# Six more projections by half products, sums kept in PSUM, and tiles moved to other start addresses

## The chip, the cores and the metric

The kernel runs on one core of one Trainium2 chip. The metric is device microseconds of one execution. Three timed runs of the kernel before gave 1398.69, 1399.0 and 1400.92 us, a median of 1399.0 us.

## The reference

One layer of a decoder with four branches, on 256 tokens of width 2048, in float32. `xn` is the normalised input; one large input matrix is cut into columns of 1024 (and four of 2048).

```
(a_q, a_k, a_v, a_g, c_b, c_c, c_h, c_g, s_q, s_k, s_v, s_g, m_q, m_g,
 i_q, i_k, i_w, r_a, r_c, r_s, r_m) = [xn @ w for w in cols]
y_a = moba_attention(a_q, a_k, a_v) * silu(a_g)        # 8 heads x 128, block branch
y_c = c_b * short_conv(c_c * c_h, conv_w, conv_b) * silu(c_g)
y_s = dsa_attention(s_q, s_k, s_v, i_q, i_k, i_w) * silu(s_g)
y_m = memory_attention(m_q, mk, mv) * silu(m_g)
merged = (sigmoid(r_a) * (y_a @ w_branch[0]) + sigmoid(r_c) * (y_c @ w_branch[1])
        + sigmoid(r_s) * (y_s @ w_branch[2]) + sigmoid(r_m) * (y_m @ w_branch[3]))
return rms_norm(x + merged @ w_out, final_g)
```

`short_conv` is a causal convolution of width 3 along the tokens, channel by channel.

## The kernel before

All weights (some 260 MB) stream once from HBM, 1 MB at a time (a tile `raw`, four buffers), on SP's queue. Every matrix product is made of three passes: ACT copies a half `raw` into `hi` (128x1024, type fp32r, line 104), DVE makes `lo = raw - hi` (line 105), both in tiles with four buffers, and PE sums hi·hi, hi·lo and lo·hi in PSUM. The activations (`x_hl`) lie split in the same way.

There are three ways to project 1024 columns:

- *Transposed* (`project_t`, lines 142 to 151): the weights are stationary, the 256 tokens move. 8 blocks of 128 columns x 16 chunks of depth x 3 passes are 384 matmuls of 256 columns. The result comes with channels on the partitions, which the attention and the convolution want. The queries, keys and gates and the convolution's four (C_C, C_H, C_B, C_G) go this way; their rows name the PSUM tile `acc`.
- *Natural* (`project`, lines 163 to 177): the activations are stationary, 512 columns of weights move. 2 halves of tokens x 2 halves of columns x 16 chunks x 3 passes are 192 matmuls of 512 columns. Rows name `r`, `v`, `w` (branch matrices) and `o` (output matrix).
- *By halves* (`by_halves`, lines 222 to 270): as natural, but over the first half of the depth the 2x2 blocks are multiplied with seven products instead of eight, from sums of activations (`x_sums`, made once) and differences of weight quarters (DVE, lines 241, 245, 251 and 261). 7x12 + 96 = 180 matmuls of 512 columns. The partial products `m` (one bank at a time) are added up in SBUF by DVE (lines 248, 249, 254, 255), then come `z`, `r`, `x` and `y` (lines 258 and 269). Seven projections go this way.

A stage of a branch is: queries, keys, values, attention (spread over the gate's projection), the gate (`to_gate`), and twice for j = 0, 1 the columns of `gate_columns` and their `merge` with the branch matrix. The first `gate_columns` of the branches M, S and A is natural, all others go by halves. The branches come in the order M, S, A, C. The order of instructions within an engine is set by the scheduler of the tile framework from the order of the code and its own estimates.

Tiles of one pool lie one behind the other. `u` (line 609) is 8x258x4 = 8256 bytes per partition, 64 more than a multiple of 128, so the tiles that lie behind it (`y`, `raw`, `hi`, `lo`) start 64 bytes off those before it (`x_hl`, `x_sums`, `mt`), counted modulo 128. The operands of a `w` matmul (`y`, `hi`) both lie behind it; those of `r`, `o` and of the halved ones lie on either side.

Of the kernel before, what the change touches and what calls it, by code (L numbers as in the profile page):

```python
# [9 lines left out]
F32 = mybir.dt.float32  # L10
# [26 lines left out]
SECTIONS_T = [(c, W) for c in (M_Q, M_G, S_Q, S_K, S_G, A_Q, A_K, A_G, C_C, C_H, C_B, C_G)]  # L37
SECTIONS_N = [(S_V, W), (A_V, W), (R_0, 4 * D)]
# [6 lines left out]
TOPK = 64  # L45


@with_exitstack
def hybrid_kernel(ctx, tc, x, xT, mem, memT, ln_g, mem_ln_g, w_t, w_n, w_idx, conv_w, conv_b, w_mem_k, w_mem_v,
# [26 lines left out]
    cb = const.tile([P, 8], F32, name="cb")  # L76
    nc.gpsimd.dma_start(out=g_x, in_=ln_g)
# [79 lines left out]
    def products(o, ah, al, hi, lo, start, stop):  # L157

        nc.tensor.matmul(o, lhsT=ah, rhs=hi, start=start, stop=False)  # L159
        nc.tensor.matmul(o, lhsT=ah, rhs=lo, start=False, stop=False)  # L160
        nc.tensor.matmul(o, lhsT=al, rhs=hi, start=False, stop=stop)  # L161
# [60 lines left out]
    def by_halves(srcs, act, sums, nat, done):  # L222
# [3 lines left out]
        (n00, n10), (n01, n11) = ([part(nat, t, n) for t in range(2)] for n in range(2))  # L226

# [38 lines left out]
        for k0 in (8, 12):
            plain((y, x), act, srcs[0], k0, (False, False), (k0 == 12,) * 2)
        for t, (o, i) in enumerate(((n00, y), (n10, x))):
            nc.vector.tensor_add(o, i, o)
# [444 lines left out]
```

## Time and profile before

| | |
|---|---|
| median of three timed runs | 1399.0 us |
| profiled execution, its own time | 1398.06 us |
| its span, first to last instruction | 1396.3 us |
| PE busy | 1380.4 us, 99% |
| DVE busy | 933.4 us, 67% |
| ACT busy | 729.2 us, 52% |
| granted TensorE clock, mean | 0.997 |

Busy time of PE counts a matmul from its start to its modelled end, and these overlap: a matmul of 256 columns has a duration of 280 ns, and the next begins 113 to 118 ns after it. So what a matmul costs is read from the distance between starts, or from a window's length over its count. A duration of DVE or ACT can be taken as it stands.

### The profile page before, as it was taken

To read this page: it belongs to the slowest core of one execution; us is meant where nothing else is said; L and a number is where in the kernel's file an instruction comes from. 1 tells how busy PE (TensorE), PEld (TensorE's weight loads), DVE (VectorE), ACT (ScalarE), POOL (GpSimd) and SP (SyncE) were. 2 spreads that over 40 slices of the span, in tenths; PEclk is the share of its full clock that TensorE was granted. 3 is DMA by queue.
4 is the path that set the end of the run, shared out by engine and by line. 5 is a ranking of instruction groups with operands and counts; after the bars stand their busy time and mean duration, and the time that the engine had idled before them with its cause. 6 is when DMAs were issued, how large, how long until landed. Compare 5 with 4: busy or idle time off the path is not lost.

```text
span 1396.3 us, 21263 instructions
## 1 busy us (share of the span) xinstructions
PE 1380.4 (99%) x8796; PEld 1243.9 (89%) x8796; DVE 933.4 (67%) x1123; ACT 729.2 (52%) x991; POOL 11.0 (1%) x25
## 2 busy tenths in 40 slices
PE   9999999999999999999999999999999999999997
PEld 9998998789998898878999899878999998878887
DVE  7687764774848884596546885487547558787654
ACT  7663675453445684354445585445343345545443
POOL 1000000000000000000000000000000000000000
PEclk9999999999999999999999999999999999999999
DMA  9774545375554735537553746537555654736551
GB/s 343 291 271 173 191 156 180 128 266 189 172 197 133 254 128 183 189 135 247 188 193 133 243 150 211 182 125 266 183 181 187 225 192 148 265 130 241 183 197 73
DMA packets 49969, 269.49 MB, mean 193 GB/s; under 512 B 6656, under 2 KB 17456, under 8 KB 19024
## 3 DMA queue, kind: packets, MB, share of 16 engines
q1 hardware_dynamic: 48960, 264.03, 55.0%
q0 software_dynamic: 624, 3.31, 0.6%
q8 instruction: 69, 1.13, 0.3%
q10 hardware_dynamic: 288, 0.79, 0.1%
q14 instruction: 28, 0.23, 0.0%
HBM read 265.88 MB, written 2.10 MB: 192 GB/s over the span
## 4 chain that ended last, share of the span: by engine, by line
PE 85%; DVE 8%; DMA 3%; issue 2%; ACT 2%; SPq 0%; POOLq 0%; POOL 0%; DVEq 0%; ACTq 0%
PE acc L138 13%; PE acc L140 13%; PE acc L139 13%; DVE lo L105 5%; PE w L160 4%; PE w L161 4%; PE w L159 4%; PE r L159 4%; PE r L161 4%; PE r L160 4%; PE o L160 2%; PE o L161 2%; PE o L159 2%; DMA raw<-in_w_n 1%; PE y L160 1%
## 5 line engine op out<-in xcount | busy, mean ns | idle before, releaser
L105 DVE TENSOR_TENSOR lo<-raw,hi 128x1024 fp32r<-128x1024 f32 (+1 forms) x538 | 640.0, 1202 | 416.5 <-ACT hi L104 414.4
L104 ACT CAST hi<-raw 128x1024 fp32r<-128x1024 f32 (+1 forms) x538 | 552.2, 1032 | 547.8 <-PE acc L139 196.4
L139 PE MATMUL acc<-x_hl,hi 128*128 128x256 f32 x1520 | 426.0, 280 | 0.0
L138 PE MATMUL acc<-x_hl,hi 128*128 128x256 f32 x1520 | 425.4, 280 | 0.5 <-ACT qt L155 0.5
L140 PE MATMUL acc<-x_hl,lo 128*128 128x256 f32 x1520 | 425.8, 280 | 0.0
L140 PEld LDWEIGHTS acc<-x_hl,lo 128*128 128x128 f32 x1520 | 288.1, 190 | 0.1
L138 PEld LDWEIGHTS acc<-x_hl,hi 128*128 128x128 f32 x1520 | 284.8, 187 | 0.9 <-ACT qt L155 0.7
L139 PEld LDWEIGHTS acc<-x_hl,hi 128*128 128x128 f32 x1520 | 284.8, 187 | 0.2
L159 PE MATMUL w<-hi,y 128*128 128x512 f32 x256 | 99.9, 390 | 0.0
L161 PE MATMUL w<-hi,y 128*128 128x512 f32 x256 | 99.7, 389 | 0.0
L160 PE MATMUL w<-lo,y 128*128 128x512 f32 x256 | 99.6, 389 | 0.0
L159 PE MATMUL r<-hi,x_hl 128*128 128x512 f32 x248 | 98.3, 396 | 0.0
L161 PE MATMUL r<-hi,x_hl 128*128 128x512 f32 x248 | 97.9, 395 | 0.0
L160 PE MATMUL r<-lo,x_hl 128*128 128x512 f32 x248 | 97.6, 394 | 0.0
L159 PEld LDWEIGHTS w<-hi,y 128*128 128x128 f32 x256 | 48.1, 188 | 10.0
L161 PEld LDWEIGHTS w<-hi,y 128*128 128x128 f32 x256 | 48.1, 188 | 10.0
L160 PEld LDWEIGHTS w<-lo,y 128*128 128x128 f32 x256 | 48.1, 188 | 9.9
L161 PEld LDWEIGHTS r<-hi,x_hl 128*128 128x128 f32 x248 | 46.7, 188 | 10.6
L160 PEld LDWEIGHTS r<-lo,x_hl 128*128 128x128 f32 x248 | 46.7, 188 | 10.4
L159 PEld LDWEIGHTS r<-hi,x_hl 128*128 128x128 f32 x248 | 46.9, 189 | 10.2
L161 PE MATMUL o<-hi,mt 128*128 128x512 f32 (+1 forms) x160 | 55.3, 347 | 0.0
L160 PE MATMUL o<-lo,mt 128*128 128x512 f32 (+1 forms) x160 | 55.1, 346 | 0.0
(246 smaller groups left out, 1860.7 us busy)
## 6 DMA issues: line engine op xcount, KB each, us to landing
raw<-in_w_t SPq DMA_DIRECT2D x92, 1024.0 KB, 5.0
raw<-in_w_n SPq DMA_DIRECT2D x80, 1024.0 KB, 4.9
raw<-in_w_branch SPq DMA_DIRECT2D x32, 1024.0 KB, 5.3
raw<-in_w_out SPq DMA_DIRECT2D x16, 1024.0 KB, 4.8
raw<-in_w_mem_k SPq DMA_DIRECT2D x8, 1024.0 KB, 6.4
raw<-in_w_mem_v SPq DMA_DIRECT2D x8, 1024.0 KB, 5.5
raw<-in_w_t SPq DMA_DIRECT2D x16, 256.0 KB, 5.9
raw<-in_memT SPq DMA_DIRECT2D x2, 1024.0 KB, 8.8
```

Source lines behind the costliest of these rows:

```text
L104: nc.scalar.copy(out=hi, in_=src)
L105: nc.vector.tensor_sub(out=lo, in0=src, in1=hi.bitcast(F32))
L138: nc.tensor.matmul(o, lhsT=hi, rhs=a[:, 0], start=(k == 0), stop=False)
L139: nc.tensor.matmul(o, lhsT=hi, rhs=a[:, 1], start=False, stop=False)
L140: nc.tensor.matmul(o, lhsT=lo, rhs=a[:, 0], start=False, stop=(k == nk - 1))
L159: nc.tensor.matmul(o, lhsT=ah, rhs=hi, start=start, stop=False)
L160: nc.tensor.matmul(o, lhsT=ah, rhs=lo, start=False, stop=False)
L161: nc.tensor.matmul(o, lhsT=al, rhs=hi, start=False, stop=stop)
```

## The change

- The block branch's queries and keys and the convolution's C_C, C_H, C_G and C_B go by halves, in natural layout. Queries, keys, the product C_C*C_H and the product C_B*silu(C_G) are then brought to channels on partitions by 16 transposes of 128x128 each (`transposed`).
- The first `gate_columns` of S and A, and two of the output matrix's four column blocks, go by halves too; for the latter, sums of the merged activations are made (`m_sums`).
- `by_halves` keeps its running sum in PSUM: `u` takes three products one on top of the other and is copied out by ACT in between; `m`, `x`, `y` go on collecting. DVE adds once for each of the four results (`finish`). Differences of weights go into tiles of their own (`held`: h1, h2), in place of a tile that is free at that time.
- Start addresses: `u`'s tile becomes 8704 bytes, a small tile `fill` shifts all that follows, and the weight parts start 64 bytes later where they are stationary. Now both operands of every 512-wide matmul start at the same place modulo 128, and those of the transposed form 64 bytes apart, as before.

```diff
-SECTIONS_T = [(c, W) for c in (M_Q, M_G, S_Q, S_K, S_G, A_Q, A_K, A_G, C_C, C_H, C_B, C_G)]
-SECTIONS_N = [(S_V, W), (A_V, W), (R_0, 4 * D)]
+SECTIONS_T = [(c, W) for c in (M_Q, M_G, S_Q, S_K, S_G, A_G)]
+SECTIONS_N = [(c, W) for c in (S_V, A_Q, A_K, A_V, C_C, C_H, C_G, C_B)] + [(R_0, 4 * D)]
+STATIONARY = 64
+    fill = const.tile([P, 56], F32, name="fill")
-    def parts_tiles(w=NB, c=NB):
-        return [spl.tile([P, 2 * NB], F32R, name=n, tag=n).rearrange("p (k c) -> p k c", c=w)[:, :, :c]
-                for n in ("hi", "lo")]
+    def parts_tiles(w=NB, c=NB, place=0):
+        i = place // 4
+        return [spl.tile([P, 2 * NB + 64], F32R, name=n, tag=n)[:, i:i + 2 * NB]
+                .rearrange("p (k c) -> p k c", c=w)[:, :, :c] for n in ("hi", "lo")]
...
-                hi, lo = parts_tiles(w, c)
+                hi, lo = parts_tiles(w, c, STATIONARY if w == TB else 0)
...
+        held = [big.tile([P, 8 // len(room) * NB], F32, name="held", tag=r) for r in room]
...
+        def finish(o, t, n):
+            p = part(nat, t, n)
+            nc.vector.tensor_add(p, o, p)
+            done(t, n, p, False)
         b11 = quarter(srcs[0], 0)
-        m1 = bank("m", tag)
-        product(m1, a(0, 0), b11, True, True)
-        nc.scalar.copy(out=n00, in_=m1)
-        z, r = bank("z", other), bank("r", other)
-        plain((z, r), act, srcs[1], 8, (True, True), (False, False))
+        u = bank("u", tag)
+        product(u, a(0, 0), b11, True, True)
+        nc.scalar.copy(out=n00, in_=u)
+        x, y = bank("x", other), bank("y", other)
+        plain((y, x), act, srcs[0], 8, True, False)
         b12 = quarter(srcs[1], 0)
-        nc.vector.tensor_sub(out=b11, in0=b12, in1=b11)
-        m5 = bank("m", tag)
-        product(m5, s(0), b11, True, True)
+        nc.vector.tensor_sub(out=h1, in0=b12, in1=b11)
+        m = bank("m", tag)
+        product(m, s(0), h1, True, True)
+        nc.scalar.copy(out=n11, in_=m)
+        plain((y, x), act, srcs[0], 12, False, False)
         b22 = quarter(srcs[1], 4)
-        nc.vector.tensor_sub(out=b11, in0=b22, in1=b11)
-        m6 = bank("m", tag)
-        product(m6, s(1), b11, True, True)
-        nc.vector.tensor_add(n10, m6, n00)
-        nc.vector.tensor_add(n01, m5, n10)
-        plain((z, r), act, srcs[1], 12, (False, False), (False, True))
-        nc.vector.tensor_sub(out=b12, in0=b22, in1=b12)
-        m7 = bank("m", tag)
-        product(m7, s(2), b12, True, True)
-        nc.vector.tensor_add(n10, m7, n10)
-        nc.vector.tensor_add(n11, m7, n01)
-        product(z, s(3), b22, False, True)
+        nc.vector.tensor_sub(out=h1, in0=b22, in1=h1)
+        product(u, s(1), h1, False, True)
+        nc.scalar.copy(out=n01, in_=u)
+        nc.vector.tensor_sub(out=h2, in0=b22, in1=b12)
+        product(u, s(2), h2, False, True)
+        nc.scalar.copy(out=n10, in_=u)
+        product(m, s(3), b22, False, False)
+        plain((m, u), act, srcs[1], 8, False, False)
         b21 = quarter(srcs[0], 4)
+        nc.vector.tensor_sub(out=h1, in0=b21, in1=h1)
+        product(x, a(1, 1), h1, False, True)
+        finish(x, 1, 0)
+        plain((m, u), act, srcs[1], 12, False, True)
+        product(y, a(1, 0), b21, False, True)
+        finish(m, 0, 1)
+        finish(u, 1, 1)
+        finish(y, 0, 0)
...
+    def transposed(nat, done):
+        for c in range(0, 8, 2):
+            pp = halves(bank("tp", "s"))
+            for i in range(2):
+                for t in range(2):
+                    nc.tensor.transpose(pp[:, i, t * P:(t + 1) * P], nat[:, t, (c + i) * P:(c + i + 1) * P], ident)
+            done(c, pp)
...
-    q = to_heads("qt", A_Q)
-    k = to_heads("kt", A_K)
+    q = to_heads("qt", A_Q, True)
+    k = to_heads("kt", A_K, True)
...
+    uu = nat_tile("uu", "vv")
+    columns(C_C, uu, kept(uu), True)
+    nat = nat_tile("ch")
+    columns(C_H, nat, times(nat, uu), True)
+    u = big.tile([P, 8 * (T + 16)], F32, name="u", tag="kt")[:, :8 * (T + 2)].rearrange("p (c t) -> p c t", c=8)
+    transposed(uu, lambda c, pp: nc.scalar.copy(out=u[:, c:c + 2, 2:], in_=pp))
...
+    bg = nat_tile("bg", "vv")
+    columns(C_G, bg, through(bg, AF.Silu), True)
+    nat = nat_tile("cb")
+    columns(C_B, nat, times(nat, bg), True)
+    y = y_parts()
+    transposed(bg, lambda c, pp: gate_parts(y, yt_tile(), pp, cc, c))
...
-    finish(BR_C, C_G, cc, (True, True), after=parts_of)
+    finish(BR_C, y, after=parts_of, last=merged_sums)
+    sums_of(lambda k0, n: mt[:, k0:k0 + n], m_sums[0])
...
+        by_halves([w_out[1], w_out[2]], lambda k: mt[:, k], m_sums[0], nat,
+                  lambda t, n, src, psum: got.append((1 + n, t, src)), ("y",))
```

`times` multiplies a result on DVE into the tile of its partner; `gate_parts` multiplies two transposed channels blocks with the convolution's result and splits them into `y`'s parts.

PE, where the halved keys' projection follows the halved queries': eight transposes of the queries (`nqt`) stand amid the products `x`, `y` and `m` of the next call.

```order
L168 MATMUL x<-hi,x_hl 128x512
L166 MATMUL y<-hi,x_hl 128x512
L166 MATMUL x<-hi,x_hl 128x512
L342 MATMUL tp<-ident,nqt 128x128 x8
L166 MATMUL m<-hi,x_sums 128x512
L167 MATMUL y<-lo,x_hl 128x512
```

Before, no transposes stood here, and nothing but matmuls of 256 columns.

PE again, in a halved call of the change: the end of the second product on `u`, one matmul of `m`, and the third product on `u`. Line 265's copy of `u` by ACT lies between the two.

```order
L166 MATMUL u<-hi,x_sums 128x512
L167 MATMUL u<-lo,x_sums 128x512
L168 MATMUL u<-hi,x_sums 128x512
L166 MATMUL m<-hi,x_sums 128x512
L166 MATMUL u<-hi,x_sums 128x512
L167 MATMUL u<-lo,x_sums 128x512
```

Before, the two products went to different banks, with matmuls of `z` and `r` ahead of the second; now the bank is the same and one matmul lies between.

DVE, where the convolution stands: first before, among the weight parts `lo` of the projection C_H, 2 + 1 + 3 instructions of it (lines 617 and 619) between parts that serve 256-wide matmuls.

```order
L614 TENSOR_TENSOR u<-acc,qt 128x256 x2
L617 TENSOR_SCALAR qt<-u,cw,cb 128x256 x2
L619 SCALAR_TENSOR_TENSOR qt<-u,cw,qt 128x256
L105 TENSOR_TENSOR lo<-raw,hi 128x1024
L619 SCALAR_TENSOR_TENSOR qt<-u,cw,qt 128x256 x3
L105 TENSOR_TENSOR lo<-raw,hi 128x1024 x3
```

Now, in the halved call for C_G, between two differences of weights (lines 266 and 263) and the third (line 272):

```order
L263 TENSOR_TENSOR held<-raw,held 128x2048
L110 TENSOR_TENSOR lo<-raw,hi 128x1024
L658 TENSOR_SCALAR cc<-u,cw,cb 128x256 x8
L110 TENSOR_TENSOR lo<-held,hi 128x1024
L660 SCALAR_TENSOR_TENSOR cc<-u,cw,cc 128x256 x2
L110 TENSOR_TENSOR lo<-held,hi 128x1024
L660 SCALAR_TENSOR_TENSOR cc<-u,cw,cc 128x256 x3
L110 TENSOR_TENSOR lo<-held,hi 128x1024
L660 SCALAR_TENSOR_TENSOR cc<-u,cw,cc 128x256 x3
L110 TENSOR_TENSOR lo<-held,hi 128x1024
L660 SCALAR_TENSOR_TENSOR cc<-u,cw,cc 128x256 x2
L272 TENSOR_TENSOR held<-raw,held 128x2048
```

All 24 instructions of the convolution (18 of them above, six behind line 272) moved from a stage of transposed projections into the middle of one halved call, between the parts that the products on `u` and `m` wait for.

## Rows read from the trace of the kernel before

**Rows 1.** The page's first part: busy time, its share of the span, instructions.

```profile
PE 1380.4 (99%) x8796; PEld 1243.9 (89%) x8796; DVE 933.4 (67%) x1123; ACT 729.2 (52%) x991; POOL 11.0 (1%) x25
```

**Rows 2.** The page's chain of work that ended last, shares of the span by engine.

```profile
PE 85%; DVE 8%; DMA 3%; issue 2%; ACT 2%; SPq 0%; POOLq 0%; POOL 0%; DVEq 0%; ACTq 0%
```

**Rows 3.** Windows cut at stage edges: from:to, length, then busy us (and instructions) of PE, PEld, DVE, ACT and POOL, granted clock, DMA share, GB/s. In order: block branch's queries and keys (transposed); the convolution's four (transposed); first gate columns of S and of A (natural, a few matmuls of edges and attention in the count); three 512-wide blocks of the output matrix.

```profile
665.40:755.80 90.40, 90.40 (x769) 90.40 (x768) 43.83 (x39) 38.02 (x49) 0.00 (x0) 1.00 0.53 181
987.10:1168.00 180.90, 180.90 (x1538) 180.90 (x1537) 100.95 (x115) 73.98 (x83) 0.54 (x1) 1.00 0.55 189
531.90:576.70 44.80, 44.80 (x195) 36.29 (x194) 20.83 (x18) 20.49 (x23) 0.00 (x0) 1.00 0.55 182
854.80:899.60 44.80, 44.80 (x194) 36.30 (x193) 20.82 (x18) 20.50 (x23) 0.00 (x0) 1.00 0.60 205
...
1300.00:1366.00 66.00, 66.00 (x294) 54.27 (x293) 36.94 (x38) 28.80 (x34) 0.00 (x0) 1.00 0.51 176
```

**Rows 4.** The same view for the seven halved projections, each cut from its first matmul to the next stage's first: one with attention matmuls in it (S_V), the longest, the shortest, and the view's last line, which sums and averages all seven.

```profile
432.90:476.00 43.10, 42.88 (x194) 35.02 (x193) 38.29 (x40) 26.52 (x32) 0.00 (x0) 1.00 0.60 208
598.50:643.60 45.10, 43.54 (x181) 34.76 (x180) 38.94 (x37) 24.36 (x25) 0.00 (x0) 0.96 0.58 198
...
1168.00:1210.40 42.40, 42.06 (x183) 33.47 (x182) 37.33 (x35) 26.08 (x29) 0.53 (x1) 1.00 0.67 236
...
sum 303.70, PE 297.93 PEld 238.73 DVE 267.38 ACT 175.44 POOL 0.53; mean PE 42.56 PEld 34.10 DVE 38.20 ACT 25.06 POOL 0.08
```

**Rows 5.** Timeline of PE, start us and duration, four pairs, each the first and the last of a run of matmuls: ten transposed ones in the convolution's stage, ten in the stage of S's queries, seven of the form `r`, seven of the form `w`.

```profile
1049.83 0.28 PE L140 MATMUL acc<-x_hl,lo 128*128 128x256 f32 x1
...
1050.89 0.28 PE L140 MATMUL acc<-x_hl,lo 128*128 128x256 f32 x1
...
399.79 0.28 PE L140 MATMUL acc<-x_hl,lo 128*128 128x256 f32 x1
...
400.81 0.28 PE L140 MATMUL acc<-x_hl,lo 128*128 128x256 f32 x1
...
549.62 0.40 PE L160 MATMUL r<-lo,x_hl 128*128 128x512 f32 x1
...
551.02 0.40 PE L160 MATMUL r<-lo,x_hl 128*128 128x512 f32 x1
...
909.82 0.39 PE L159 MATMUL w<-hi,y 128*128 128x512 f32 x1
...
911.18 0.39 PE L159 MATMUL w<-hi,y 128*128 128x512 f32 x1
```

**Rows 6.** Groups of instructions by line in the window 1168.0 to 1210.4, one halved call (DVE, then ACT): parts, a difference of weights, an addition onto the result, ACT's part, ACT's copy out of PSUM. Columns: busy us, mean ns of one, idle before.

```profile
L105 DVE TENSOR_TENSOR lo<-raw,hi 128x1024 fp32r<-128x1024 f32 x23 | 27.3, 1220 | 4.7 <-ACT hi L104 4.6
...
L245 DVE TENSOR_TENSOR raw<-raw 128x2048 f32<-128x2048 f32 x1 | 2.3, 2285 | 0.0
...
L249 DVE TENSOR_TENSOR sig<-m,sig 128x512 f32<-128x512 f32 x1 | 0.7, 684 | 0.0
...
L104 ACT CAST hi<-raw 128x1024 fp32r<-128x1024 f32 x22 | 22.5, 1050 | 14.5 <-PE x L161 4.6 <-DVE raw L245 4.3 <-PE r L161 2.9
...
L237 ACT COPY sig<-m 128x512 f32<-128x512 f32 x1 | 0.6, 587 | 0.3 <-PE m L161 0.3
```

**Rows 7.** The same view of DVE over the convolution's projections, 986 to 1166: its parts, the two kinds of convolution instruction, and a gate's product and part.

```profile
L105 DVE TENSOR_TENSOR lo<-raw,hi 128x1024 fp32r<-128x1024 f32 x64 | 78.4, 1226 | 79.1 <-ACT hi L104 79.1
L619 DVE SCALAR_TENSOR_TENSOR qt<-u,cw,qt 128x256 f32<-128x256 f32 x16 | 7.0, 478 | 0.0
...
L617 DVE TENSOR_SCALAR qt<-u,cw,cb 128x256 f32<-128x256 f32 x8 | 2.9, 406 | 0.0
...
L341 DVE TENSOR_TENSOR yt<-yt,qt 128x512 f32<-128x512 f32 x3 | 2.1, 685 | 0.0
L105 DVE TENSOR_TENSOR y<-yt,y 128x512 fp32r<-128x512 f32 x3 | 2.1, 685 | 0.0
```

**Rows 8.** Timeline of PE at four transposes of the merged result (one line for all four, start and length over all) and the two matmuls behind them.

```profile
1306.56 0.60 PE L633 MATMUL pp<-ident,merged 128*128 128x128 f32 x4
1306.92 0.48 PE L159 MATMUL o<-hi,mt 128*128 128x512 f32 x1
1307.23 0.39 PE L160 MATMUL o<-lo,mt 128*128 128x512 f32 x1
```

**Rows 9.** Inside the longest halved call: PE's timeline at its first wait; the clock of the 8 us around it (PE alone); what ACT waited for in that stage (waits, total us, times, longest).

```profile
609.23 0.39 PE L161 MATMUL m<-hi,x_sums 128*128 128x512 f32 x1
610.42 0.51 PE L159 MATMUL m<-hi,x_sums 128*128 128x512 f32 x1 [0.81 <-ACT hi L104]
...
609.00:617.00 8.00, 6.44 (x20) 0.79 0.13 22
...
ACT sig L237 <- DVE merged L499: 4.5, 1, 4.5
```

**Rows 10.** The page's DMA issues: KB each, median us from issue to landing.

```profile
raw<-in_w_n SPq DMA_DIRECT2D x80, 1024.0 KB, 4.9
```

More of the change, by code (lines that the diff above doesn't have):

```diff
@@ L155, in copy_t, with products @@
             nc.scalar.activation(out=dst[:, j], in_=a[:rows], func=func)
[L157 to L161, printed above, removed]
+    def products(o, ah, al, hi, lo, start, stop, **kw):
+        nc.tensor.matmul(o, lhsT=ah, rhs=hi, start=start, stop=False, **kw)
+        nc.tensor.matmul(o, lhsT=ah, rhs=lo, start=False, stop=False, **kw)
+        nc.tensor.matmul(o, lhsT=al, rhs=hi, start=False, stop=stop, **kw)
     def project(src, act, name, t_outer=False):
@@ L209, in product @@
             al = a(k)
-            products(o, al[:, 0], al[:, 1], hi, lo, start and k == 0, stop and k == 3)
+            products(o, al[:, 0], al[:, 1], hi, lo, start and k == 0, stop and k == 3, skip_group_check=True)
     def plain(o, act, src, k0, start, stop):
@@ L216, in plain, with by_halves @@
                 a = act(k0 + k)[:, :, t * P:(t + 1) * P]
-                products(o[t], a[:, 0], a[:, 1], hi, lo, start[t] and k == 0, stop[t] and k == 3)
+                products(o[t], a[:, 0], a[:, 1], hi, lo, start and k == 0, stop and k == 3, skip_group_check=True)
     def part(nat, t, n):
         return nat[:, t, n * NB:(n + 1) * NB]
-    def by_halves(srcs, act, sums, nat, done):
+    def by_halves(srcs, act, sums, nat, done, room):
         tag = next(turn)
@@ L266, in by_halves @@
[L266 to L269, printed above, removed]
-            done(t, 0, o, False)
+        u = bank("u", tag)
[3 more added lines that the diff above has]
+        plain((y, x), act, srcs[0], 8, True, False)
+        b12 = quarter(srcs[1], 0)
+        nc.vector.tensor_sub(out=h1, in0=b12, in1=b11)
@@ L295, in x_act, with columns @@
         return x_hl[:, k]
-    def columns(c0, nat, done, halved, srcs=None):
+    def columns(c0, nat, done, halved, srcs=None, room=("y",)):
         if srcs is None:
@@ L301, in columns @@
         if halved:
-            return by_halves(srcs, x_act, x_sums, nat, done)
+            return by_halves(srcs, x_act, x_sums, nat, done, room)
         for n in range(2):
@@ L320, in through, with times, done, to_heads @@
         return done
-    def to_heads(name, c0):
-        dst = big.tile([P, 8, T], F32, name=name, tag=name)
-        for b in range(4):
-            copy_t(dst[:, 2 * b:2 * b + 2], project_t(w_t[FIRST[c0] + b], x_act))
+    def times(nat, dst):
+        def done(t, n, src, psum):
+            nc.vector.tensor_mul(part(dst, t, n), src, part(dst, t, n))
+        return done
+    def transposed(nat, done):
[5 more added lines that the diff above has]
+            done(c, pp)
+    def to_heads(name, c0, halved):
+        dst = big.tile([P, 8, T], F32, name=name, tag=name)
+        if not halved:
+            for b in range(4):
+                copy_t(dst[:, 2 * b:2 * b + 2], project_t(w_t[FIRST[c0] + b], x_act))
+            return dst
+        nat = nat_tile("n" + name)
+        columns(c0, nat, kept(nat), True)
+        transposed(nat, lambda c, pp: nc.scalar.copy(out=dst[:, c:c + 2], in_=pp))
         return dst
@@ L479, in gate_columns @@
         sig = nat_tile("sig")
-        columns(None, sig, through(sig, AF.Sigmoid), halved, [w_n[FIRST[R_0] + 4 * b + 2 * j + n] for n in range(2)])
+        columns(None, sig, through(sig, AF.Sigmoid), halved, [w_n[FIRST[R_0] + 4 * b + 2 * j + n] for n in range(2)],
+                room=("kt", "vv"))
         return sig
@@ new lines, in blocks_of, with block @@
+    def blocks_of():
+        def block(n):
+            c0, c = blocks[n]
+            acc = project(w_out[c0 // NB][:, :, c0 % NB:c0 % NB + c], lambda k: mt[:, k], "o", t_outer=(n == last))
+            return ((n, t, acc[t]) for t in range(2))
+        yield from block(0)
+        got = []
+        nat = nat_tile("no")
+        by_halves([w_out[1], w_out[2]], lambda k: mt[:, k], m_sums[0], nat,
+                  lambda t, n, src, psum: got.append((1 + n, t, src)), ("y",))
+        yield from got
+        for n in range(3, last + 1):
+            yield from block(n)
```

107 lines of the change are left out of this document (51 added, 56 removed).

## Prediction

> **What bounds the kernel now.** I read the page's busy times and its chain first. PE is busy for 1380.4 us of a span of 1396.3 [rows 1], and 85% of the chain that ended last is PE, with DVE at 8% and DMA at 3% [rows 2]. So the time is the number of matmuls times the distance between their starts, plus what PE waits, and a change is worth what it takes out of that. Since durations of PE overlap, I then read the distances from the timeline of PE [rows 5], and the lengths of stages from windows cut at their edges [rows 3, 4]. Last come the engines that feed PE: the groups of DVE and ACT in one halved call [rows 6], and the place where a halved call waits most [rows 9].
>
> Distances. A transposed matmul of 256 columns starts (1050.89 - 1049.83)/9 = 0.118 us after the one before in the convolution's stage, and (400.81 - 399.79)/9 = 0.113 in the stage of S's queries [rows 5]: the same instruction has two paces, and the projections that this change removes run at the slow one: 90.4 us for 768 matmuls and 180.9 for 1536 are 0.1177 and 0.1178 each [rows 3]. A 512-wide matmul takes (551.02 - 549.62)/6 = 0.233 in the form r, and (911.18 - 909.82)/6 = 0.227 in the form w [rows 5]; the output matrix's 288 take 66.0 us, 0.229 each [rows 3]. Per column, 512-wide ones are a little cheaper than the slow 256-wide ones: 1024 columns of weights cost 45.2 us transposed (90.4/2), 44.8 natural [rows 3], and 42.4 to 45.1 by halves, 303.7/7 = 43.4 on average [rows 4].
>
> Waits. 180 matmuls at 0.229 are 41.2 us, so halved calls lose 1.2 to 3.9 us today. In the longest, PE waited for ACT and DVE twice, first after 609.23, and the granted clock over those 8 us averaged 0.79: a part of them ran at 1.2 instead of 2.4 GHz [rows 9]. DVE is the cause: it is busy for 38.2 us of a halved call on average [rows 4], 88% of it, against 100.95 of 180.9 in the transposed stage [rows 3].
>
> **The change, part by part.** All against the profiled execution's own time, 1398.06 us, which is 0.9 below the median of 1399.0.
>
> 1. *Removed:* six transposed projections, 90.4 + 180.9 = 271.3 us [rows 3].
>
> 2. *Added:* six halved calls. The step of a matmul is now one for operands that start at the same place modulo 128. Of the 512-wide forms before only w is like that, and it is the quickest, so I take 0.2267: 180 x 0.2267 = 40.8 us. For waits I put 1.6 us per call. The lower end is 0, the upper 3.9 as today's worst. Two things pull against each other. Four of eight additions per call go, 4 x 0.684 = 2.7 us of DVE [rows 6], which leaves 35.5 us of its 38.2, and differences have tiles of their own, so a weight buffer is free sooner for a DMA that takes 4.9 us [rows 10]. But the third product on u must wait until ACT has copied the second's sum out of the same bank: 0.587 for the copy [rows 6] and 0.39 - 0.23 = 0.16 from the next start to the end of the last matmul, whose duration is 0.39 [rows 9], less the one matmul of m that the order puts between, 0.23: about 0.5 us in every call. It can't be below that unless the scheduler's gap is wider than shown, and the rest, 1.1, is the smallest loss seen today. Behind the waiting copy, on ACT, stand the casts of the coming parts (1.05 each [rows 6]), for which DVE and then PE wait; the eleven other matmuls of m, 2.5 us, cover two casts. So 42.4 us per call, 254.4 for six. This is the term that I am least sure of: 0 gives 244.8, 3.9 gives 268.2.
>
> 3. *Transposes:* 64. Four take 1306.92 - 1306.56 = 0.36 us, and the matmul behind them 0.31 instead of 0.23, so 0.44 for four [rows 8] and 7.0 us in all. They stand amid the next call's products, where their sources are long done. The bounds are 0.09 and 0.15 each (duration 0.60 for four), 5.8 to 9.6. The Trainium skill (TensorE: Matmul & The Clock Gate, Part 4: PE-mode transpose) gives about 275 ns for a 128x128 transpose inside a kernel. The durations here agree, but the starts lie a third of that apart, so the trace decides; with 275 ns in sequence the term would be 17.6 us and the sum 10.6 higher.
>
> 4. *First gate columns of S and A:* 2 x (44.8 - 42.4) = -4.8 us [rows 3].
>
> 5. *The seven old halved calls:* 303.7 us, of which the two with attention in them hold some 13 further matmuls each, 1.3 us a call [rows 4]. 303.7 - 2.6 - 7 x 42.4 = 4.3 gained, by the new step and the PSUM sums.
>
> 6. *Output matrix:* 66.0 [rows 3] becomes 96 x 0.2267 + 42.4 = 64.2: -1.8. The sums of merged activations are DVE work of some 8 us (2 of 1.22 and 8 of 0.684 by [rows 6]) beside the first block's 21.8 us of matmuls; if that cover fails, the halved call waits for up to 8.
>
> 7. *Other 512-wide matmuls* that are now aligned (values of M and its first gate columns, 384): 384 x (0.2292 - 0.2267) = -1.0.
>
> 8. *DVE in the convolution's stage.* Before, the 24 convolution instructions (16 x 0.478 + 8 x 0.406 = 10.9 us) ran where DVE sat idle for 79.1 us waiting for ACT [rows 7]. Now they stand in the call for C_G, in the stretch of three differences (2.29 each [rows 6]) and eight parts that feeds the four quick products of 2.7 us. That call then has 35.5 + 10.9 = 46.4 us of DVE against 40.8 of PE. Behind it, the gate's products and parts (4 x 0.685 twice = 5.5 us [rows 7]) fall into the next call, and C_H and C_B each bring four multiplications, 2.7 us. DVE can run ahead by four part tiles only, so I let half of 16.4 = 10.9 + 5.5 us reach PE: +8. The bounds are 0 and 16.4.
>
> Transposed projections that stay keep their pace: 0.
>
> Sum: -271.3 + 254.4 + 7.0 - 4.8 - 4.3 - 1.8 - 1.0 + 8.0 = -13.8 us. 1398.06 - 13.8 = 1384.3, and with the 0.9 to the median 1385. What ends last stays PE, but DVE rises from 933.4 by 54 more parts (66), 36 more differences (82) and some 10, to about 1090 of 1385, 79%.
>
> **The rivals.**
>
> *Placement brings nothing.* In the trace, w at 0.227 and r at 0.233 differ in more than their start addresses: in the stage, and in what ran before; and a transposed matmul has two paces at the same addresses. For it: the pace alone can change without any move. Against it: w is at 0.227 wherever I looked. Without placement a step stays at 66.0/288 = 0.2292 [rows 3]: 16 x 180 x 0.0025 = 7.2, and 1.0 of point 7, so 1393. The Trainium skill (SBUF — State Buffer, Who interferes with whom) has PE read the moving operand and the weights through two independent ports and never wait on anyone; by that rule, an address should not matter, and this rival is the forecast.
>
> *DVE and ACT take the lead: slower.* The place is every halved call, at the second and third product on u, where three quick products follow two differences. If PE waits there twice for about 1 us, as after 609.23, and its clock falls to half each time, a call costs 45.1 as the longest today [rows 4]. In all 16 that is 16 x 2.7 = 43 us, 1428; in half of them 1407. It decides from a mean call of 42.4 + 13.8/16 = 43.3 on, which is today's mean. For it: in the longest call, ACT waited 4.5 us for the merge ahead of it before its first copy [rows 9], and eight calls (three of the block branch, five of the convolution's) now have no transposed projection with idle DVE between them. Against it: 2.7 us less of DVE in each.
>
> *The waits go.* If the freed buffers and the saved additions hide all but the copy of u, 0.6 us a call, and the convolution's cost is 4: 16 us and 4 less, 1365. For it: the shortest call today already loses only 1.2, with more additions. Against it: point 8's stretch.
>
> **How the numbers follow.** Forecast (1372 to 1394, centre 1385): 0.57. Placement brings nothing, 1393: 0.10. Waits go, 1350 to 1372: 0.18. Slower, above 1402: 0.15. No change is what lies within 0.2% of 1399.0, 2.8 us, about what a measurement of this kernel tells from none. Faster: 0.57, 0.18 and half of the placement case, 0.05, make 0.80; the same: 0.05 from the placement case and 0.01 from the slower one's lower edge; slower 0.14. The range leaves out 0.1 on either side: 1358 to 1404.
>
> **What would show it.** Right: 512-wide starts 0.227 apart in every form; 16 halved calls of 42 to 43 us, with a gap of some 0.5 us before the third product on u; C_G's call longer than its neighbours; the transposed rest unchanged. Wrong: gaps of 1 us and more with a granted clock below 1 in many calls, ACT waiting for merges, or 0.23 in forms that are aligned. If the four quick products show no gap in C_G's call, DVE's load was not the limit, and the time should come out near 1375.

## The result and the profile after

The changed kernel takes 1381.9 us (median of 4 runs, 1381.5 to 1386.2) against 1400.0 before (4 runs): a ratio of 0.988, 95% interval 0.986 to 0.990, so it is faster by some 18 us. 1385 had been forecast. The profiled execution has a span of 1380.5 us, 15.8 below the 1396.3 of before.

The page of after, its busy times and its chain by engine [rows 1, 2 of before]:

```profile
PE 1354.7 (98%) x7600; PEld 1178.9 (85%) x7600; DVE 1076.6 (78%) x1223; ACT 817.3 (59%) x1094; POOL 11.2 (1%) x26
...
PE 39%; DVE 3%; ACT 1%; issue 1%; POOLq 0%; POOL 0%; DVEq 0%; ACTq 0%
```

DVE has risen from 67% to 78%, 1077 us where about 1090 was forecast. Of the chain only some 44% is listed, so it says less than before; the windows say more. Here are eight of the sixteen halved calls, from each one's first matmul to the next stage's first (columns as in [rows 3]): S's first gate columns, S's second ones (the longest before [rows 4]), A's values, the convolution's C_C, C_G and C_B, C's first gate columns, the output matrix's; and the view's sum over all sixteen.

```profile
530.30:572.40 42.10, 41.71 (x187) 34.18 (x186) 34.11 (x29) 29.23 (x35) 0.00 (x0) 1.00 0.54 190
594.20:635.70 41.50, 41.10 (x181) 33.68 (x180) 35.05 (x31) 25.58 (x29) 0.00 (x0) 1.00 0.54 189
743.00:789.50 46.50, 44.41 (x209) 36.73 (x208) 38.81 (x40) 29.65 (x38) 0.00 (x0) 1.00 0.52 181
972.30:1014.40 42.10, 41.39 (x181) 33.60 (x180) 37.62 (x32) 24.80 (x26) 0.00 (x0) 1.00 0.55 200
1056.00:1106.80 50.80, 46.04 (x197) 35.86 (x196) 47.00 (x58) 28.73 (x32) 0.00 (x0) 0.97 0.47 166
1106.80:1148.40 41.60, 41.21 (x182) 33.75 (x181) 37.47 (x33) 26.38 (x29) 0.00 (x0) 1.00 0.56 202
1148.40:1198.30 49.90, 45.92 (x198) 37.32 (x197) 43.05 (x42) 28.82 (x34) 0.57 (x1) 0.93 0.54 190
...
1308.70:1350.20 41.50, 41.11 (x181) 33.72 (x180) 36.32 (x34) 26.46 (x33) 0.00 (x0) 1.00 0.56 196
sum 693.00, PE 676.40 PEld 551.93 DVE 595.32 ACT 430.51 POOL 1.75; mean PE 42.28 PEld 34.50 DVE 37.21 ACT 26.91 POOL 0.11
```

Thirteen calls lie between 41.5 and 43.3 (some hold 5 to 17 neighbouring matmuls, as the count behind PE shows). Three do not: 46.5, 50.8 and 49.9. What PE waited for, over the whole span (total us, times, longest):

```profile
PE u L166 <- ACT hi L109: 4.2, 3, 3.5
PE u L166 <- ACT vv L265: 2.5, 2, 2.1
PE u L166 <- ACT sig L265: 2.4, 6, 0.4
PE m L167 <- DVE lo L110: 2.2, 2, 1.9
PE u L167 <- DVE lo L110: 1.9, 4, 0.7
```

L265 is the copy of u between its second and its third product. It comes back in fifteen of the sixteen calls, under the name of that call's result; in C's first gate columns a longer wait for `hi` stands in its place. The timeline shows the typical one, in A's second gate columns (PE at the first matmul of u's second product, at the one matmul of m, and at the first of u's third product; ACT's copy):

```profile
925.25 0.39 PE L166 MATMUL u<-hi,x_sums 128*128 128x512 f32 x1
...
927.97 0.44 PE L166 MATMUL m<-hi,x_sums 128*128 128x512 f32 x1
928.17 0.58 ACT L265 COPY sig<-u 128x512 f32<-128x512 f32 x1 [0.30 <-PE u L168]
...
928.81 0.50 PE L166 MATMUL u<-hi,x_sums 128*128 128x512 f32 x1 [0.40 <-ACT sig L265]
...
929.15 0.39 PE L167 MATMUL u<-lo,x_sums 128*128 128x512 f32 x1
```

Twelve matmuls of u take (927.97 - 925.25)/12 = 0.227 each, the step of w in [rows 5]. Then u's next one starts 0.84 after m's instead of 0.23, and the one behind it 0.11 late: 0.72 us. 180 x 0.2267 + 0.72 = 41.5 is the length of a call with nothing else in it. The long ones have something of their own. A's values hold 29 neighbouring matmuls (16 transposes of the keys, 13 of the attention), and the copy stands behind an attention step on ACT (the loading of a function table and two exponentials), so that PE waits 2.1 us for it:

```profile
764.59 1.28 ACT L412 ACT_TABLE_LOAD   x1
...
766.78 0.56 ACT L265 COPY vv<-u 128x512 f32<-128x512 f32 x1
```

In C_G's call 24 convolution instructions stand between DVE's parts. All of the 2.2 us above and 1.4 of the 1.9 for which PE waited for `lo` fall into it. The groups of DVE in 1056.0 to 1106.8 (count, then busy us and mean ns):

```profile
L660 DVE SCALAR_TENSOR_TENSOR cc<-u,cw,cc 128x256 f32<-128x256 f32 x16 | 7.0, 488 | 0.0
L658 DVE TENSOR_SCALAR cc<-u,cw,cb 128x256 f32<-128x256 f32 x8 | 2.7, 413 | 0.0
```

In C's first gate columns the difference h2 goes into the tile from which the gate's product `bg` is still being transposed (`room=("kt", "vv")`), and begins only behind the last of those transposes:

```profile
1168.81 0.60 PE L342 MATMUL tp<-ident,bg 128*128 128x128 f32 x4
1169.45 2.29 DVE L266 TENSOR_TENSOR held<-raw 128x2048 f32<-128x2048 f32 x1 [0.43 <-PE tp L342]
...
1172.92 0.79 PE L166 MATMUL u<-hi,x_sums 128*128 128x512 f32 x1 [3.51 <-ACT hi L109]
...
1174.78 0.63 PE L168 MATMUL u<-hi,x_sums 128*128 128x512 f32 x1
1175.20 0.63 PE L166 MATMUL u<-hi,x_sums 128*128 128x512 f32 x1
```

PE stands for 3.5 us and again for 0.5, and then runs 0.43 us a matmul until 1179: the granted clock of this call is 0.93, a part of it at the lower level, 1.2 GHz.

### The profile page after: what moved, and what is told of

It is laid out like the page before. It is cut to its first block, busy times and chain, and to the rows that moved or that the text cites. A ratio compares the mean times of both kernels' runs of the same rounds, so it can differ in the third digit from the quotient of the medians.

```text
span 1380.5 us, 19110 instructions
## 1 busy us (share of the span) xinstructions
PE 1354.7 (98%) x7600; PEld 1178.9 (85%) x7600; DVE 1076.6 (78%) x1223; ACT 817.3 (59%) x1094; POOL 11.2 (1%) x26
## 5 line engine op out<-in xcount | busy, mean ns | idle before, releaser
L110 DVE TENSOR_TENSOR lo<-raw,hi 128x1024 fp32r<-128x1024 f32 (+1 forms) x464 | 551.0, 1199 | 251.8 <-ACT hi L109 249.7
L145 PE MATMUL acc<-x_hl,hi 128*128 128x256 f32 (+1 forms) x752 | 211.6, 281 | 0.0
L146 PE MATMUL acc<-x_hl,hi 128*128 128x256 f32 (+1 forms) x752 | 210.3, 280 | 0.0
L147 PE MATMUL acc<-x_hl,lo 128*128 128x256 f32 (+1 forms) x752 | 210.1, 280 | 0.0
L109 ACT CAST hi<-held 128x1024 fp32r<-128x1024 f32 x128 | 132.1, 1054 | 44.5 <-PE x L168 23.6
L110 DVE TENSOR_TENSOR lo<-held,hi 128x1024 fp32r<-128x1024 f32 x128 | 151.9, 1221 | 7.2 <-ACT hi L109 6.8
L146 PEld LDWEIGHTS acc<-x_hl,hi 128*128 128x128 f32 (+1 forms) x752 | 141.1, 188 | 0.2
L145 PEld LDWEIGHTS acc<-x_hl,hi 128*128 128x128 f32 (+1 forms) x752 | 141.0, 188 | 0.2
L147 PEld LDWEIGHTS acc<-x_hl,lo 128*128 128x128 f32 (+1 forms) x752 | 140.8, 187 | 0.1
L166 PE MATMUL u<-hi,x_hl 128*128 128x512 f32 x180 | 70.3, 391 | 0.7 <-ACT bg L268 0.7
L168 PE MATMUL u<-hi,x_hl 128*128 128x512 f32 x180 | 70.3, 390 | 0.0
L166 PE MATMUL y<-hi,x_hl 128*128 128x512 f32 x180 | 70.2, 390 | 0.0
L168 PE MATMUL y<-hi,x_hl 128*128 128x512 f32 x180 | 70.1, 389 | 0.0
L166 PE MATMUL x<-hi,x_hl 128*128 128x512 f32 x180 | 70.1, 389 | 0.0
L168 PE MATMUL x<-hi,x_hl 128*128 128x512 f32 x180 | 70.1, 389 | 0.0
```

The costliest lines, as they stand in the source:

```text
L109: nc.scalar.copy(out=hi, in_=src)
L110: nc.vector.tensor_sub(out=lo, in0=src, in1=hi.bitcast(F32))
L145: nc.tensor.matmul(o, lhsT=hi, rhs=a[:, 0], start=(k == 0), stop=False)
L146: nc.tensor.matmul(o, lhsT=hi, rhs=a[:, 1], start=False, stop=False)
L147: nc.tensor.matmul(o, lhsT=lo, rhs=a[:, 0], start=False, stop=(k == nk - 1))
L168: nc.tensor.matmul(o, lhsT=al, rhs=hi, start=False, stop=stop, **kw)
```

## Experiments

The times are medians; each run is timed beside the kernel before on its chip, and the ratio to it follows with its 95% interval. The lengths of calls are from windows as above.

**e1_swap.** One product is moved.

```diff
-        nc.vector.tensor_sub(out=h2, in0=b22, in1=b12)
-        product(u, s(2), h2, False, True)
-        nc.scalar.copy(out=n10, in_=u)
         product(m, s(3), b22, False, False)
+        nc.vector.tensor_sub(out=h2, in0=b22, in1=b12)
+        product(u, s(2), h2, False, True)
+        nc.scalar.copy(out=n10, in_=u)
```

> The changed kernel with one line moved: the product s(3) x b22 on m stands between the second and the third product on u, not behind the third. Nothing else differs, the sums are the same. Theory (the copy of u stands bare in every call): in the profile of after each of the 16 halved calls has one gap of 0.61 us before u's third product and 0.11 behind it, 0.72 x 16 = 11.5 us. With twelve matmuls of m (2.7 us) between, the copy is covered: 1382 - 11.5 = 1370.5, between 1368 and 1373, and the typical call falls from 42.0 to 41.3. Rival (DVE is what feeds the quick products, and the gap only hides its lateness): the parts of b22 are now wanted first and h2 right behind, the gap comes back elsewhere in the call as a wait for lo, and the time stays within 3 us of 1382.

Measured: 1370.2 us, 0.979 (0.977 to 0.980), 11.7 below after. Undisturbed calls last 40.8, which is 180 x 0.2267 and nothing else; every call lost 0.3 to 2.1. A's values lost the 2.1 (46.5 to 44.4), and PE no longer waits for anything there: the copy behind the exponentials is covered too. The timeline of PE in A's second gate columns, where u runs through:

```profile
919.43 0.39 PE L166 MATMUL u<-hi,x_sums 128*128 128x512 f32 x1
919.66 0.39 PE L166 MATMUL m<-hi,x_sums 128*128 128x512 f32 x1
919.88 0.39 PE L167 MATMUL u<-lo,x_sums 128*128 128x512 f32 x1
```

So the bare copy was the largest single loss of the change, and DVE was early enough to feed the other order.

**e2_pool.** The convolution on GpSimd (`nc.vector` to `nc.gpsimd`, a multiply-add as a multiplication and an addition).

> The changed kernel with the convolution's arithmetic on GpSimd instead of DVE (40 instructions of 256 columns); its place in the program stays. Theory (point 8 of the prediction: the convolution's 10.9 us of DVE stand between the differences and parts of C_G's call, and about 9 us of them reach PE): C_G's call falls from 50.8 to 42 to 43, the half clock inside it goes, and the time is 1382 - 8 = 1374 (1372 to 1376). Rival (DVE's load isn't the limit there; the long call is ACT's, whose copies and casts stand behind each other): C_G's call stays above 48, and the time between 1380 and 1384. A third way: GpSimd beside DVE slows DVE's parts; then the groups of lo in that call are longer than 1.22 us.

Measured: 1383.3 us, 0.988 (0.986 to 0.989), no gain. C_G's call, C_B's and C's first gate columns:

```profile
1057.30:1100.70 43.40, 43.01 (x198) 35.34 (x198) 39.66 (x33) 28.68 (x32) 31.69 (x16) 1.00 0.54 194
1100.70:1145.10 44.40, 42.97 (x181) 33.11 (x180) 40.81 (x31) 26.39 (x29) 43.98 (x24) 1.00 0.53 190
1145.10:1199.60 54.50, 48.42 (x197) 38.54 (x196) 45.85 (x44) 28.64 (x34) 3.27 (x2) 0.91 0.49 174
```

C_G's call does nearly what the theory said, 50.8 to 43.4. But GpSimd is busy for 78.9 us with what took DVE 9.7, and it still reads `u` when the first difference of weights of C's first gate columns is due. That goes into u's tile (`room=("kt", "vv")`) and waits for GpSimd's last reading of it; PE then waits for DVE's additions behind it:

```profile
1144.40 2.83 DVE L257 TENSOR_TENSOR held<-raw 128x2048 f32<-128x2048 f32 x1 [1.73 <-POOL ct L661]
...
1147.97 0.47 PE L166 MATMUL y<-hi,x_hl 128*128 128x512 f32 x1 [1.12 <-DVE cb L247]
```

The granted clock of that call falls to 0.91, and the wait for h2 comes on top, 3.5 us as in after. The third way shows too: beside GpSimd the parts from `raw` take 1298 ns in C_G's call and 1371 in C_B's, instead of 1224. The Trainium skill (SBUF — State Buffer, Who interferes with whom) says that a DVE instruction with two SBUF inputs contends with a GpSimd instruction that reads SBUF; this fits.

**e3_inpl.** In branch C the gate's product overwrites `cc` instead of using `yt`'s one buffer.

```diff
-    transposed(bg, lambda c, pp: gate_parts(y, yt_tile(), pp, cc, c))
+    transposed(bg, lambda c, pp: gate_parts(y, cc[:, c:c + 2], pp, cc, c))
```

> The changed kernel with the product silu-gate x convolution written over the convolution's own tile (cc) instead of the one buffer yt, in branch C alone. Theory (the 3.7, 1.0 and slower-clock loss in C's first gate call is a buffer wait: the difference h2 goes into the tile from which bg is still being transposed, and these transposes wait for one another through yt): the four transposes and their products follow each other at once, h2 starts some us earlier, and the call falls from 49.9 to 42 to 44, so 1382 - 6.5 = 1375.5 (1374 to 1378). Rival (DVE is simply late there, with the gate's parts on top): the same instructions stand before h2 on DVE, the call stays above 48, 1380 to 1383.

Measured: 1382.6 us, 0.988 (0.986 to 0.989); the call lasts 49.8. A miss. The timeline shows why:

```profile
1158.04 1.03 PE L342 MATMUL tp<-ident,bg 128*128 128x128 f32 x8
1160.78 1.28 DVE L364 TENSOR_TENSOR cc<-tp,cc 128x512 f32<-128x512 f32 x2
1165.28 1.03 PE L342 MATMUL tp<-ident,bg 128*128 128x128 f32 x8
1167.94 1.28 DVE L364 TENSOR_TENSOR cc<-tp,cc 128x512 f32<-128x512 f32 x2
1169.13 2.28 DVE L266 TENSOR_TENSOR held<-raw 128x2048 f32<-128x2048 f32 x1
```

The products are together now, but the second eight transposes still come 7 us behind the first, in the order of PE, for there are two PSUM banks for four groups. The chain through `yt` was not what held h2.

**e4_nopl.** The new start addresses are undone alone (no `fill`, `STATIONARY = 0`, `u` of 8256 bytes).

> The changed kernel without the new start addresses: no fill tile, weight parts without their 64 bytes, u's tile 8256 bytes again. The order of work is the same. Theory (the step of a 512-wide matmul is set by whether its two operands start at the same place modulo 128): the halved calls' and the output matrix's steps go from 0.227 to 0.229 or up to 0.233, w stays at 0.227: 2900 x 0.0025 = 7 to 2900 x 0.006 = 17 us more, 1389 to 1399. Rival (placement brings nothing, the step came with the order of work or the stage): 0.227 stays everywhere, 1381 to 1383.

Measured: 1385.8 us, 0.990 (0.988 to 0.992), 3.9 above after, between the two ranges that were expected. A's second gate columns last 42.0 instead of 41.6, and so in all undisturbed calls. Worked out over all starts in the traces, the 512-wide x and y go from 0.2268 to 0.2291 us, and w stays at 0.2267 to 0.2269. Over the 3360 steps of all forms but w that is 6.6 us, waits left out. But the 2640 transposed steps fall from 115.4 to 114.7 ns (1.9 us) and the output matrix's two half blocks from 117.8 to 113.3 (0.9). So the edit of the addresses moves both widths, in opposite directions. For 512 columns it is the distance of the operands; the operands of the 256-wide ones are 64 bytes apart in both kernels, so their change has another cause, not known. The 3.9 is not the steps alone either: in this profile A's values took 48.3 us instead of 46.5, at a granted clock of 0.96.

**e5_banks.** e1_swap, and `bg`'s four groups of transposes go into the banks `s`, `s`, `pp`, `yp`.

> e1_swap, and the four groups of transposes of branch C's gate (bg) go into four PSUM banks (two of them idle in this branch) instead of two in turn. In e3_inpl the gate's products followed each other, yet the last transposes still stood behind the second product on u in PE's order, since a bank must be emptied before the third group, and h2 (whose tile bg is) began only after them. Theory (C's first gate call waits for a tile: h2 after the last transpose after a free bank): with four banks all 16 transposes stand early in that call, h2 is made before it is needed, and the call falls from 49.1 to 41 to 43; 1370.2 - 7 = 1363 (1361.5 to 1365). Rival (DVE is late there whatever the tile, by the gate's products and parts): the call stays above 47, 1368 to 1371.

Measured: 1366.2 us, 0.977 (0.975 to 0.978), 4.0 below e1_swap and a little above the range that was expected. The transposes and the difference in C's first gate columns, and that call's window:

```profile
1145.54 1.03 PE L342 MATMUL tp<-ident,bg 128*128 128x128 f32 x8
1150.51 1.03 PE L342 MATMUL tp<-ident,bg 128*128 128x128 f32 x8
1152.95 2.28 DVE L267 TENSOR_TENSOR held<-raw 128x2048 f32<-128x2048 f32 x1
```

```profile
1139.40:1183.10 43.70, 43.22 (x197) 35.30 (x196) 42.65 (x42) 29.31 (x34) 0.57 (x1) 1.00 0.59 206
```

h2 begins 14 us into the call, where it began 21 in in after and 23 in in e1_swap; the call falls from 49.1 to 43.7 with 42.7 us of DVE in it, hardly less than the 43.0 of e1_swap, and the clock is whole. So it was the tile, not DVE's load. The total gains less than the call: C_G's call, where the edit changes nothing, took 51.7 instead of 50.4 in this profile, at a clock of 0.93.

**e6_conv.** e1_swap, and channels 4 to 7 of the convolution are queued on DVE behind C_G's last addition.

> e1_swap, and the convolution of channels 4 to 7 is queued on DVE behind the last addition of C_G's call, so that 12 of its 24 instructions (5.5 us) fall into C_B's call. Theory (point 8: DVE's load between the quick products is what C_G's call waits for, and each call can hide some 5 us): C_G's call falls from 50.4 to 43 to 45, C_B's rises by at most 2 from 41.0; 1370.2 - 5 = 1365 (1363 to 1367). Rival (as e2_pool's result read on its face: what is taken out of C_G's call is paid in the two calls behind it): the sum of C_G, C_B and the first gate call stays within 1.5 of 140.5, 1369 to 1372.

Measured: 1369.8 us, 0.979 (0.978 to 0.980): no gain. The rival was right:

```profile
1047.30:1094.80 47.50, 45.04 (x197) 36.35 (x196) 42.56 (x45) 28.75 (x32) 0.00 (x0) 0.96 0.50 177
1094.80:1139.80 45.00, 41.82 (x182) 33.56 (x182) 41.84 (x45) 26.38 (x29) 0.00 (x0) 1.00 0.53 187
1139.80:1187.70 47.90, 44.79 (x197) 36.41 (x196) 42.89 (x42) 28.89 (x34) 0.57 (x1) 0.96 0.55 198
```

140.4 in sum against 140.5. C_B's call, undisturbed with 37.4 us of DVE, loses 4 with 41.8. These calls have no room of 5 us.

**e7_cback.** After, with the convolution's four projections transposed again.

> The changed kernel (not e1_swap) with the convolution's four projections transposed again, as in the kernel before, the rest of the change kept. Theory (these four calls, 42.2 + 41.6 + 50.8 + 41.6 = 176.2, and the 7 to 8 us that the first gate call behind them loses, are no cheaper than the 180.9 of the transposed stage): the time falls a little, 1382 - 3 = 1379 (1377 to 1381). The prediction's own terms (four calls of 42.4, 3.5 for transposes, 8 for DVE against 180.9) give 1382. Rival (halving a projection pays wherever it is done, 2.8 us a call): 1382 + 8 = 1390.

Measured: 1381.1 us, 0.988 (0.986 to 0.989): the time of after, at the upper end of the theory's range and near the 1382 of the prediction's own terms. Their window is that of before to the tenth [rows 3], and the first gate columns behind them fall to 41.6:

```profile
974.50:1155.40 180.90, 180.90 (x1538) 180.90 (x1537) 100.90 (x115) 74.11 (x83) 0.00 (x0) 1.00 0.56 188
```

In this version the convolution's halves gain nothing: in after the four calls take 176.1 and the gate columns 8.3 more, 3.5 on the losing side. A's values, which the edit doesn't touch, took 48.1 here and not 46.5, at a granted clock of 0.96 instead of 1.00, which hides half of that.

**e8_all.** e5_banks and e6_conv together.

> e5_banks and e6_conv together. If the tile wait and DVE's load are two separate losses, their gains add: 1370.2 - 7 - 5 = 1358 (1356 to 1361), with no halved call above 45. If the convolution's second half, now just ahead of the gate, makes DVE late in the first gate call, the gain is that of e5_banks alone or less, 1363 to 1366.

Measured: 1364.5 us, 0.976 (0.974 to 0.978). The gains don't add; it is e5_banks within the interval. The reason that was expected for this is not the one: C's first gate columns last 43.9, as in e5_banks. C_G's call falls to 46.1 from 51.7, but C_B's rises to 45.0 from 41.0.

**e9_noconv.** e5_banks without the 16 multiply-adds.

> e5_banks without the convolution's 16 multiply-adds (taps 0 and 1 are left out, so the output is another): 7.6 of its 10.9 us of DVE go. Theory (point 8: it is DVE's load between the quick products that C_G's call waits for): C_G's call falls from 51.7 to 42 to 44 and nothing comes back behind it, 1366.2 - 9 = 1357 (1356 to 1359); then e2_pool's and e6_conv's missing gain was a late result or a second place without room, not another cause. Rival (C_G's call waits for ACT, whose casts stand behind its copies out of u and m): it stays above 48, 1364 to 1367.

Measured: 1359.3 us, 0.972 (0.971 to 0.974), 7 below e5_banks and just above the expected range. C_G's call:

```profile
1047.10:1091.60 44.50, 43.34 (x197) 35.30 (x196) 40.71 (x42) 28.65 (x32) 0.00 (x0) 1.00 0.53 189
```

16 x 0.488 = 7.8 us less of DVE, 7.2 us less of the call than in e5_banks, where the granted clock of this call was 0.93, and 5.9 less than in e1_swap, where it was 1.00 as here. So most of the convolution's time on DVE reaches PE there, and nothing comes back behind it: C_B's call takes 41.0 and C's first gate columns 43.9.

**e10_act.** e8_all with the convolution's first step on ACT (`nc.scalar.activation`, `AF.Identity`).

> e8_all with the convolution's first step (8 instructions, 2.7 us) on ACT in place of DVE. Theory (DVE's load): C_G's call falls from 46.1 to about 44 and C_B's from 45.0 to about 43.5, 1364.5 - 3 = 1361.5 (1360 to 1363). Rival (eight more instructions on ACT delay the casts as much): 1364 to 1367.

Measured: 1364.1 us, 0.975 (0.974 to 0.976). C_G's and C_B's calls are 45.4 and 43.9 instead of 46.1 and 45.0; the total can't be told from e8_all's and lies where the rival had put it. It has the lowest median of the complete versions, 18 us below after and 34 below the kernel before on its chip, and two thirds of what it adds to the change come from e1_swap.

**e11_stat0** and **e12_stat32.** Only the place of the stationary weight parts changes: `STATIONARY = 0` on e8_all, `STATIONARY = 32` on e10_act.

> e8_all, but the stationary weight parts of the transposed projections start at the same place modulo 128 as the tokens that move past them, instead of 64 bytes later; the 512-wide forms are not touched. If the rule found for 512 columns held for 256, the mean step of acc would fall from 115.4 to about 113.3 ns: 2640 x 0.0021 = 5.5 us less, 1359. If 256 columns want the other placement (the output matrix's half blocks went from 113.3 to 117.8 ns when they were aligned): acc rises to about 117.8, 6.3 us more, 1371. If the two paces of a transposed matmul have another cause, 1363 to 1366.

> e10_act with the stationary weight parts of the transposed projections (and the output matrix's two half blocks, which share their tiles) 32 bytes off the tokens' place modulo 128 instead of 64. Steps of acc so far: 119.8 ns at 0 (e11_stat0), 115.4 at 64, the latter a mixture of stretches at 113.3 and at 117.8. If only the very same place is slow for 256 columns, acc stays at 113 to 116 and the time between 1358 and 1365. If the step depends on the distance, between 0 and 64, acc comes to 116 to 119.8: 2 to 12 us more than e10_act's 1364, 1366 to 1376.

Measured: 1377.3 us, 0.984 (0.983 to 0.986), and 1370.6 us, 0.979 (0.978 to 0.981); 13 and 6.5 above their bases (11.5 and 5.7 by the ratios, since the bases were timed on other chips). Over all transposed stages the mean step is 119.8 ns in e11_stat0 and 118.2 in e12_stat32, where the bases have 115.4. e11_stat0 lies above all that was expected; e12_stat32 is as expected if the step depends on the distance. The first transposed stage, 384 matmuls, in e10_act (64 bytes), e12_stat32 and e11_stat0:

```profile
28.70:72.20 43.50, 43.50 (x386) 43.50 (x385) 27.49 (x35) 31.46 (x48) 1.62 (x1) 1.00 0.83 295
```

```profile
28.60:74.00 45.40, 45.40 (x386) 45.40 (x385) 27.95 (x35) 31.37 (x48) 1.63 (x1) 1.00 0.80 283
```

```profile
29.60:75.70 46.10, 46.10 (x387) 46.10 (x386) 28.29 (x35) 31.45 (x48) 1.63 (x1) 1.00 0.77 272
```

0.113, 0.118 and 0.120 us a matmul: for 256 columns the same place is the slow one and 64 bytes off the quick one, the reverse of 512 columns. In other stages the 64 bytes run at 0.118 too; at 0 and 32 one pace holds throughout. The expectation of e11_stat0 misread the half blocks: they share the tiles that are shifted, and were 64 bytes apart before and after.

## Why the prediction was right, and where not

The sum gave 1384.3 for the profiled execution, which took 1382.3 by its own time: 13.8 us of gain forecast, 15.8 measured, and a mechanism (PE sets the time; fewer matmuls, a quicker step, some waits) that held. By its points:

1. Removed: as told. e7_cback brings back the 180.9.
2. Added: 261.6 (42.2, 43.3, 42.1, 41.6, 50.8, 41.6). The 254.4 of the forecast leave out what other points put into the same windows: 32 of point 3's transposes (3.5 us, in A's keys and in C_G's call) and 5.5 of point 8, together 263.4. The gap before u's third product is 0.72 instead of 0.5 with the late matmul behind it. The 1.1 put beside it is not there: calls without neighbours lose 0.7 in all. So the 1.6 us of waits a call was 0.9 too much, and this is the term that was mis-sized in most calls.
3. Transposes: each lasts 272 ns, close to the 275 of the Trainium skill (TensorE: Matmul & The Clock Gate, Part 4: PE-mode transpose), but eight take 1.03 us from the first's start to the last's end, so they start far less than that apart; the trace's 0.11 each holds.
4. First gate columns of S and A: 42.1 each, -5.4 (forecast -4.8).
5. The seven old calls: 305.7, so +2.0 where -4.3 was forecast. Most of this is a matter of where things are counted: the other 32 transposes (3.5 us) and the gate's half of point 8 (2.7) stand in A's values and C's first gate columns, and with them the terms for these seven come to 305.6. That the two agree is luck. Five calls came out 0.6 to 0.9 below their terms, 4.0 in all; A's values came out 1.0 above (46.5 against 45.5) and C's first gate columns 3.0 above (49.9 against 46.9). The term took all seven down to one typical length and looked at no single call's tiles and queues, so neither cause is in it: the copy behind the attention's exponentials on ACT, which e1_swap shows, and a tile that is still being read, which e5_banks shows.
6. Output matrix: 22.7 + 41.5 = 64.2, as forecast; the sums of the merged activations are hidden.
7. Too small to tell.
8. DVE in the convolution's stage: C_G's call took 50.8 against 49.6 by the terms. e9_noconv shows that 5.9 to 7.2 of 7.8 us reach PE there, more than the half that was let through. Of the gate's 5.5 little does: with the tile free (e5_banks) C's first gate columns take 43.7, of which 40.8 are the call's matmuls and 1.8 its transposes.

The transposed projections that stay had been put at 0. By their steps they rose by some 1.5 us (M's gate most, from 114.7 to 116.9 ns), and the output matrix's half blocks by 0.9.

The rival by which DVE and ACT take the lead had named the place (second and third product on u) but not what happened: the gap is the copy, 0.72 us at a full clock, and the longest call of before, 45.1, is now 41.5. The rival by which the waits go (0.6 us a call) is the nearer one for most calls; the three long ones kept the time from it. The rival of placement falls: x and y go from 226.8 to 229.1 ns when the addresses are undone. But the kernel loses 3.9 us by it, half of the 8.2 priced, since the 256-wide steps give back 2.8. The rule of the Trainium skill that the rival rested on (SBUF — State Buffer, Who interferes with whom: independent ports, PE never waits), read as the prediction read it, does not agree with these two steps. Over all sixteen calls 16 x 42.4 + 2.6 + 7.0 + 8.0 = 696.0 had been forecast and 693.0 came: thirteen calls lie some 8 us below their terms in all and three 5 us above, so the total was nearer than its parts.

Where did the 15.8 us come from? Six projections 271.3 to 261.6 (-9.7), first gate columns -5.4, output matrix -1.8, other 512-wide ones about -1, old calls +2.0. Of the -9.7, 4.9 are A's queries and keys, 4.8 the convolution's four, and the latter are lost again in C's gate columns (e7_cback). The gain also hangs on the pace of what was removed: those 2304 matmuls ran at 0.118 us; at 0.113, the other pace of the same form, they would have taken 261 (an estimate), as much as the six calls do.

Open: why C_G's call differs between e1_swap and e5_banks, and what more than DVE's load (1.2 us of waits in e9_noconv) is in it. No run undoes the running sums in PSUM alone, or the halving of A's queries and keys alone; what these are worth is read from windows.

## What to carry to other kernels

A sum kept on in PSUM saves additions, but here each read of it between two products stood bare until another product was put between; that order was worth 12 us, two thirds as much as the whole change. A tile lent to a new user is a wait on its last reader, wherever the scheduler has put that reader (h2 behind the transposes of `bg`, and in e2_pool behind GpSimd). Work on a loaded engine can be moved only where a neighbouring call has room. The sum of busy time does not tell it: C_B's call lost 4 us with 41.8 us of DVE (e6_conv), C's first gate columns about 1 with 42.7 (e5_banks). It seems to matter which products the work stands ahead of; no run tests that alone.

## What was not expected of the hardware

- The step of a matmul depends on where its two operands start, counted modulo 128 bytes, and on its width: 512 columns take 0.2267 us at the same place and 0.229 at 64 bytes off; 256 columns take 0.120 at the same place, 0.118 at 32 bytes off, and 0.113 or 0.118 at 64. Whether 128 is the right modulus no run tells.
- At 64 bytes off, 256-wide ones run at these two paces in stretches of hundreds. In after, 0.118 at 333 us and 0.113 at 350, in the same form:

```profile
332.92 0.28 PE L145 MATMUL acc<-x_hl,hi 128*128 128x256 f32 x1
...
334.10 0.28 PE L146 MATMUL acc<-x_hl,hi 128*128 128x256 f32 x1
...
349.58 0.28 PE L147 MATMUL acc<-x_hl,lo 128*128 128x256 f32 x1
...
350.71 0.28 PE L145 MATMUL acc<-x_hl,hi 128*128 128x256 f32 x1
```

Ten steps take 1.18 us, and ten 1.13. No run here tells the cause.
- GpSimd took 78.9 us for the convolution's 24 instructions' worth of work (in 40), against 9.7 on DVE.
